# A hybrid decoder layer on one core: places in SBUF of the matmuls' two operands

## The chip, the cores and the metric

The kernel runs on one core of a Trainium2 chip. The metric is the device time of one execution in microseconds, taken as the median of several runs. PE is TensorE's matmul side, PEld its weight loads, DVE is VectorE, ACT ScalarE, POOL GpSimd and SP SyncE, which starts the transfers.

## The reference, cut to what matters

One layer is computed for 264 tokens (256 of a prompt and 8 single ones with states), all in float32:

```
xn = rms_norm(x, g_mix)                       # 2048 wide
z  = xn @ w_in                                # 3584 columns: pool 512 | lru 1024 | gelu gate 1024 | glu 512 + 512
y_pool = pool_mixer(...) @ w_pool_br          # 512 -> 2048, with a 4 x 128 x 128 map in it
y_lru  = (rg_lru(conv(u_lru)) * gelu(u_gel)) @ w_lru_br   # 1024 -> 2048, with 2 x 8 gate blocks of 128 x 128
y_conf = silu(layer_norm(conv(glu))) @ w_conf_br          # 512 -> 2048
gates  = sigmoid(xn @ w_gate + b_gate)        # 2048 -> 3 x 2048
x = x + (g_a * y_pool + g_b * y_lru + g_c * y_conf) @ w_out
x = x + square(relu(rms_norm(x, g_mlp) @ w_up)) @ w_down  # 2048 -> 8192 -> 2048
return rms_norm(x, g_final), the new states
```

## The kernel before

Tokens lie along the free axis, channels on the 128 partitions. Every product is made of k tiles: 128 input channels by 512 output columns of weights, which are four weight tiles (m = 0 to 3) of 128 x 128, against one operand tile of 128 x 264. Weights and operand are both split into a high and a low part in fp32r, and `mm3` makes each product of three matmuls (whi and x high, wlo and x high, whi and x low). So a k tile is 12 matmuls, and TensorE executes 11,405 of these and a few others.

The weights come in chunks of two k tiles (1024 floats a partition) through the ring `raw` of six. `split` writes a chunk's high part with ACT (`nc.scalar.copy`, L228) into `whi` and the rest with DVE (L229) into `wlo`, three chunks ahead of the matmuls; both hold four chunks. `weight_plan` lists 67 groups (a weight matrix, its k tiles, 512 columns) and their 478 chunks, and the main loop walks that list: it splits chunk i + 3, issues the matmuls of chunk i, evacuates the four accumulators at a group's end, and then lets `run_bg` issue work of three queues (lru, pool, conf) by a budget of cost for each engine. Everything stands in the order in which this program issues it; nothing else reorders it.

Where the operands lie is deliberate. An operand tile isn't stored in one piece: `pieces` puts its 264 columns in 33 pieces of 8 floats (32 bytes), 32 floats (128 bytes) apart, with 4 floats more after every 11 pieces. So four operand tiles fit between each other, and tile k lies `k % 4 * 8` floats to the right of the first, tiles of the next four in another set (`k // 4 * SET`, 2208 floats), the low part 1088 floats behind the high one. `both` gives the two access patterns. `turn` shifts the whole by 16 floats for each unit (for most operands 0 or 32 floats). Such tiles are `A` (the normed input, later the merged branches, and half of the MLP's hidden tiles), `L` and `LH` (the LRU's conv output, then its result), `Q` (pool and conformer results) and `xn2` (the MLP's input, four buffers; the profile calls them xn). The hidden tiles of every other quarter of the MLP lie in LH and Q.

The weight slots are 520 floats (2080 bytes) long, two for a chunk: each next k tile of weights begins 32 bytes further modulo 256. `weight_plan` picks, among the chunks of a group that are left, the first whose place fits the operand's place, `(c + turn - len(chunks)) % NHI == 0`, and the first that is left when none does. That makes the order of k in many groups a rotated one. The LRU's gate blocks (four chunks of 512 floats, kind "lru", evacuated by ACT with a sigmoid in `lru_gate_mm`, L517 and L518) and the pool's map (kind "grp") stand between the chunks of a group, at the positions that `LRU_AT` names.

Of the kernel before, what the change touches and what calls it, by code (L numbers as in the profile page):

```python
# [15 lines left out]
P = 128  # L16
# [3 lines left out]
N = TP + TS  # L20
# [27 lines left out]
STRETCH = 11  # L48
STEP = 32
HOP = STRETCH * STEP + 4  # L50
LOW = 1088
SET = 2208
SKEW = 20
A_SIZE = 8896
B_SIZE = 2496
L_SIZE = 4480
SLOT = 520
HEAD = N + 512
FIRST = 8
CH = 1024  # L60
NRAW = 6
NHI = 4
LRU_AT = (1, 3, 4, 4)
WARM = 17
LEAD = 4
SINGLE = 16
# [5 lines left out]
    return KD + c * (2 * N + CH)  # L72


def turn_of(name, k0):

    return 0 if name in ("w_in", "w_gate", "w_conf_br") else 2


def weight_plan():

    groups = [("w_in", 0, 16, m) for m in (1, 2, 0, 3, 4, 6, 5)]
    for g in range(4):
        groups += [("w_gate", 0, 16, t) for t in ((0, 4, 1), (5,), (2, 6), (3, 7))[g]]
        groups += [("w_pool_br", 0, 4, g), ("w_lru_br", 0, 8, g)]
    groups += [("w_gate", 0, 16, 8 + g) for g in range(4)]  # L90
    groups += [("w_conf_br", 0, 4, g) for g in range(4)]
    groups += [("w_out", 0, 16, m) for m in range(4)]
    for q in range(4):
        groups += [("w_up", 0, 16, q * 4 + m) for m in range(4)]
        groups += [("w_down", q * 16, 16, m) for m in range(4)]
    chunks = []
    for gi, (name, k0, k, m) in enumerate(groups):
        left, turn = list(range(k // 2)), turn_of(name, k0)
        for at in range(k // 2):
            c = next((c for c in left if (c + turn - len(chunks)) % NHI == 0), left[0])  # L100
            left.remove(c)
            chunks.append(("dense", gi, c, CH, at == 0, not left))
            for g in [g for g in range(4) if (name, m, at) == ("w_in", 4, LRU_AT[g])]:
                chunks.append(("lru", g, 0, 512))
            if (name, m) == ("w_gate", 0) and at == 3:
                chunks += [("grp", 0, 0, 512), ("none", 0, 0, 0)]
    return groups, chunks

# [2 lines left out]
def hybrid_step(ctx: ExitStack, tc: tile.TileContext, first, par_in, st_in, wall, y_out, st_out):  # L111
# [7 lines left out]


    raw = cpool.tile([P, NRAW, CH], F32, name="raw")
    whi = cpool.tile([P, 2 * NHI, SLOT], F32R, name="whi")
    wlo = cpool.tile([P, 2 * NHI, SLOT], F32R, name="wlo")
    par = cpool.tile([P, NPAR], F32, name="par")
    rstd = cpool.tile([P, N], F32, name="rstd")
    a_all = cpool.tile([P, A_SIZE], F32R, name="A")
# [15 lines left out]
        a, b = PCOL[name]  # L142
        return par[:, a:b] if i is None else par[:, a + i:a + i + n]

    def pieces(t, k, a, turn):
        at = SKEW + a + k // 4 * SET + k % 4 * OCT + turn * 2 * OCT
        return bass.AP(tensor=t.tensor, offset=t[:, at:].offset,
                       ap=[list(t.ap[0]), [HOP, N // (STRETCH * OCT)], [STEP, STRETCH], [1, OCT]])

    def high(t, k, turn=0):  # L150
        return pieces(t, k, 0, turn)

    def low(t, k, turn=0):
        return pieces(t, k, LOW, turn)

    def both(t, k, turn=0):
        return high(t, k, turn), low(t, k, turn)

    def v(t):
        return t.rearrange("p (a b c) -> p a b c", b=STRETCH, c=OCT)  # L160
# [7 lines left out]
        return psum.tile([P, 512], F32, name="acc", tag="acc")  # L168

    def w_tile(i, kt, m):  # L170
        at = 2 * (i % NHI) + kt
        return whi[:, at, m * P:(m + 1) * P], wlo[:, at, m * P:(m + 1) * P]

    spare = nc.const_aps.tensor(1.0, [P, 2 * P], dtype=mybir.dt.bfloat16)
    Gf = G.rearrange("p a n -> p (a n)")
# [45 lines left out]
    def split(j, half=None):  # L221
        if j >= len(chunks) or not chunks[j][3]:
            return
        a, b = (0, chunks[j][3] // 512) if half is None else (half, half + 1)
        at = 2 * (j % NHI)
        r = raw[:, j % NRAW, :].rearrange("p (k c) -> p k c", k=2)[:, a:b, :]
        h, lo = whi[:, at + a:at + b, :512], wlo[:, at + a:at + b, :512]
        nc.scalar.copy(h, r)  # L228
        nc.vector.tensor_tensor(lo, r, f(h), op=ALU.subtract)  # L229

    def head_half(k, h):

        s = slice(h * 256, h * 256 + 256)
        return whi[:, k, s], wlo[:, k, s], head_w(k)[:, s]

    def cast_head(k, h):
        hi, _, w = head_half(k, h)
# [116 lines left out]

    def x_high(k):
        if k < 2:
            nc.vector.tensor_scalar(high(a_all, k), v(x_of(k)), gm[:, k:k + 1], None, op0=ALU.mult)  # L357
        else:
            nc.scalar.activation(high(a_all, k), v(x_of(k)), AF.Copy, scale=gm[:, k:k + 1])

    def x_low(k):
        rest_of(both(a_all, k), x_of(k), gm[:, k:k + 1])

    def x_tile(k):
        x_high(k)
# [144 lines left out]
    def lru_gate_mm(ct, c, j):  # L510
        assert "xc" in done
        out = []
        for t in range(2):
            ps = acc()
            mm3(ps, w_tile(c, 0, 2 * j + t), both(L, ct), True, True)
            out.append(ps[:, :N])
        nc.scalar.activation(RA[:, ct, :], out[0], AF.Sigmoid, bias=pv("b_lru_a", ct))  # L517
        nc.scalar.activation(TM[:, ct, :], out[1], AF.Sigmoid, bias=pv("b_lru_x", ct))  # L518
        spend(act=1.0)
        if ct % 2:  # L520
            def times():
                nc.vector.tensor_tensor(XC[:, ct - 1:ct + 1, :], XC[:, ct - 1:ct + 1, :], TM[:, ct - 1:ct + 1, :],
                                        op=ALU.mult)
                spend(dve=0.71)

            later(1, times)
# [101 lines left out]
    def conf():  # L628
# [77 lines left out]
        stage(q, "dve", 0.3, [lambda ct=ct: affine(ct) for ct in g4])  # L706
        stage(q, "pool", 0.7, [lambda ct=ct: mul(ct) for ct in g4])
        mark(q, "swished")
        stage_split(q, 4, lambda c: both(Q(), 4 + c), lambda c: VC[:, c, :])
        mark(q, "conf")  # L710


# [16 lines left out]
    def pooling():  # L729
# [25 lines left out]
        stage("pool", "pool", 2.0, [lambda i=i: add(i) for i in range(4)])  # L755
        stage("pool", "pool", 0.3, [rows], 0)
        stage("pool", "dve", 0.8, [lambda gi=gi: diff(gi) for gi in range(4)])
        stage_split("pool", 4, lambda c: both(Q(), c, 2), lambda c: DU[:, c, :])
        mark("pool", "pool")

    def grp_mm(c):
        assert "pool" in done
        for gi in range(4):
            ps = acc()
            mm3(ps, w_tile(c, 0, gi), both(Q(), gi, 2), True, True)
            nc.scalar.activation(DU[:, gi, :], ps[:, :N], AF.Copy, scale=pv("pool_scale", gi))
        stage_split("pool", 4, lambda c: both(Q(), c, 2), lambda c: DU[:, c, :])
        mark("pool", "grp")


# [2 lines left out]
    def bpart(k):  # L773
        if not M:
            M.extend(cpool.tile([P, B_SIZE], F32R, name=f"xn2{i}", tag=f"B{i}") for i in range(4))
        return both(M[k // 4], k % 4, 2 + 2 * (k // 4 % 2))

    def gate_tile(br, g, m):
        if br == 2:
# [20 lines left out]
    def branch_evac(br, g, m, ps):  # L800
        assert "grp" in done and (br < 1 or "lru" in done) and (br < 2 or "conf" in done)
        t = gate_tile(br, g, m)
        k = g * 4 + m
        nc.vector.tensor_tensor(t, ps[:, :N], t, op=ALU.mult)
        spend(dve=0.43)
        if br == 1:
            nc.gpsimd.tensor_tensor(partial(k), t, gate_tile(0, g, m), op=ALU.add)
            spend(pool=0.8)
        if br == 2:
            nc.gpsimd.tensor_tensor(t, t, partial(k), op=ALU.add)  # L810
            spend(pool=0.8)
            later_split(*both(a_all, k, 2), t, 3, 2)

    def later_split(hi, lo, x, n, gap):
        def one():
# [39 lines left out]

    def hid(q, k):
        if q % 2 == 0:
            return both(a_all, k, 2)
        return both(LH() if k < 8 else Q(), k % 8, 2)

    def up_evac(q, m, ps):
        hi, lo = hid(q, m)
# [37 lines left out]
    def group(gi):  # L900
        name, k0, _, m = groups[gi]
        if name == "w_in":
            def rhs(i):
                return both(a_all, i)
            fn = {0: pool_evac, 1: lru_x_copy, 2: lambda c, p: lru_x_evac(4 + c, p), 3: gel_evac,
                  4: lambda c, p: gel_evac(4 + c, p), 5: ca_evac, 6: cb_evac}[m]
            return rhs, fn
        if name == "w_gate":
            return (lambda i: both(a_all, i)), (lambda c, p: gate_evac(m // 4, m % 4, c, p))
        if name == "w_pool_br":  # L910
            assert "grp" in done
            return (lambda i: both(Q(), i, 2)), (lambda c, p: branch_evac(0, m, c, p))
        if name == "w_lru_br":
            assert "lru" in done
            return (lambda i: both(LH(), i, 2)), (lambda c, p: branch_evac(1, m, c, p))
        if name == "w_conf_br":
            assert "conf" in done
            return (lambda i: both(Q(), 4 + i)), (lambda c, p: branch_evac(2, m, c, p))
        if name == "w_out":
            return (lambda i: both(a_all, i, 2)), (lambda c, p: out_evac(m * 4 + c, p))  # L920
        if name == "w_up":
            return bpart, (lambda c, p: up_evac(m // 4, (m % 4) * 4 + c, p))
        q = k0 // 16
# [2 lines left out]
    def after(gi):  # L926

        name, _, _, m = groups[gi]
        if name == "w_in":
            if m == 2:  # L930
                lru_conv(range(4, 8))
                lru_conv_sample()
                mark("lru", "conv")
                stage_split("lru", 8, lambda c: both(L, c), lambda c: XC[:, c, :])
                mark("lru", "xc")
            elif m == 5:
                conf()
# [2 lines left out]
            elif m in (3, 4):  # L940
                if m == 4:
                    gelu(0)
                    gelu(2)
                    stage_split("lru", 8, lambda c: both(LH(), c, 2), lambda c: GEL[:, c, :])
                    mark("lru", "lru")

    def by_operand(i, kt, rhs, pss):
# [22 lines left out]
    for i, ch in enumerate(chunks):  # L970
# [19 lines left out]
        if kind == "dense":  # L990
            rhs, fn = group(gi)
            name = groups[gi][0]
            start, end = ch[4:]
            if start:
                pss = [acc() for _ in range(4)]
            if i < len(chunks) - 2:
# [105 lines left out]
def _stream(w):  # L1102
    groups, chunks = weight_plan()
    out = np.zeros((len(chunks) // 2, P, 2, CH), w["w_in"].dtype)
    blocks = np.stack([w["w_lru_a"], w["w_lru_x"]], 1)
    for i, (kind, gi, c, n, *_) in enumerate(chunks):
# [75 lines left out]
```

## Time and profile before

| | us |
|---|---|
| median of 3 runs | 1321.48 (1321.29 to 1322.16) |
| the profiled execution, its own time | 1321.26 |
| its span, first to last instruction | 1319.2 |
| PE busy | 1308.6 (99%) |
| DVE busy | 841.7 (64%) |
| ACT busy | 720.1 (55%) |

A row of the timeline has the start in us from the span's start, the length of the merged instructions, engine, line, operation, output tile, then the operands and the count; matmuls of one line merge only while their operands' names stay the same, so a row changes from whi to wlo and back. Matmuls overlap in the pipeline: their length is some 0.28 us, and the distance from start to start is what the stream costs. A window's row has the length, busy time, and behind x the instructions that touch the window.

### The profile page before, as it was taken

How to read it: one execution, taken by the hardware profiler on the slowest of the kernel's cores; microseconds unless marked ns; L12 is line 12 of the kernel's file. 1: busy time of each engine (PE TensorE's matmuls, PEld its weight loads, DVE VectorE, ACT ScalarE, POOL GpSimd, SP SyncE). 2: the span in 40 equal slices, each digit the busy share in tenths (PEclk: the TensorE clock that was granted, in tenths of full speed). 3: DMA queues.
4: the chain of work that ended last, by engine and by line, in shares of the span. 5: the costliest groups of instructions: out<-in, count | busy, mean ns of one | idle time of the engine just before them, and what ended most of it. 6: DMA issues, size and time to landing. Idle time of an engine off the chain costs nothing.

```text
span 1319.2 us, 26550 instructions
## 1 busy us (share of the span) xinstructions
PE 1308.6 (99%) x11421; PEld 1306.0 (99%) x11421; DVE 841.7 (64%) x1130; ACT 720.1 (55%) x1035; POOL 100.6 (8%) x125
## 2 busy tenths in 40 slices
PE   9999999999999999999999999999999999999997
PEld 9999999999999999999999999999999999999996
DVE  8787888776777668666655455655455645465554
ACT  7668577667675645455544334543344533354544
POOL 0230010110102014021000000000000000000012
PEclk9999999999999999999999999999999999999999
DMA  8656556555575555555555555555555555555552
GB/s 330 212 192 211 173 188 224 193 192 192 192 224 192 192 192 193 192 192 192 192 192 192 192 194 192 193 194 192 193 192 193 194 195 194 192 194 195 195 193 76
DMA packets 40821, 257.48 MB, mean 195 GB/s; under 512 B 4480, under 2 KB 6784, under 8 KB 11776
## 3 DMA queue, kind: packets, MB, share of 16 engines
q1 hardware_dynamic: 40272, 255.19, 56.3%
q8 instruction: 89, 1.46, 0.4%
q10 hardware_dynamic: 432, 0.61, 0.1%
q14 instruction: 28, 0.23, 0.0%
HBM read 252.57 MB, written 3.21 MB: 194 GB/s over the span
## 4 chain that ended last, share of the span: by engine, by line
PE 97%; DVE 1%; ACT 0%; DMA 0%; issue 0%; DVEq 0%
PE acc L245 97%; DVE A L165 1%; DMA tmp<-first_dram 0%; DVE y L1068 0%; ACT whi L228 0%; DVE wlo L229 0%; DVE wlo L242 0%; ACT tmp L517 0%; DVE A L357 0%; ACT tmp L518 0%; DVE acc L1059 0%; DVEq L1159 0%; DVE G L1058 0%; DVE acc L1057 0%; PE acc L1045 0%
## 5 line engine op out<-in xcount | busy, mean ns | idle before, releaser
L229 DVE TENSOR_TENSOR wlo<-raw,whi 128x1024 fp32r<-128x1024 f32 (+1 forms) x478 | 584.7, 1226 | 454.6 <-ACT whi L228 451.3
L228 ACT CAST whi<-raw 128x1024 fp32r<-128x1024 f32 (+1 forms) x478 | 494.1, 1036 | 541.0 <-PE acc L245 495.8
L245 PE MATMUL acc<-A,whi 128*128 128x264 f32 x3968 | 679.9, 276 | 0.0
L245 PEld LDWEIGHTS acc<-A,whi 128*128 128x128 f32 x3968 | 597.1, 188 | 0.4 <-ACT whi L238 0.4
L245 PE MATMUL acc<-A,wlo 128*128 128x264 f32 x1984 | 540.9, 275 | 0.2
L245 PEld LDWEIGHTS acc<-A,wlo 128*128 128x128 f32 x1984 | 370.1, 187 | 0.9 <-DVE wlo L229 0.9
L245 PE MATMUL acc<-xn,whi 128*128 128x264 f32 x2048 | 350.9, 275 | 0.0
L245 PEld LDWEIGHTS acc<-xn,whi 128*128 128x128 f32 x2048 | 308.3, 187 | 0.0
L245 PE MATMUL acc<-xn,wlo 128*128 128x264 f32 x1024 | 280.8, 274 | 0.0
L245 PEld LDWEIGHTS acc<-xn,wlo 128*128 128x128 f32 x1024 | 191.9, 187 | 0.0
L245 PE MATMUL acc<-Q,whi 128*128 128x264 f32 x776 | 136.6, 277 | 0.0
L245 PE MATMUL acc<-LH,whi 128*128 128x264 f32 x768 | 133.3, 275 | 0.0
L245 PEld LDWEIGHTS acc<-Q,whi 128*128 128x128 f32 x776 | 118.2, 187 | 0.0
L245 PEld LDWEIGHTS acc<-LH,whi 128*128 128x128 f32 x768 | 116.4, 187 | 0.0
L245 PE MATMUL acc<-Q,wlo 128*128 128x264 f32 x388 | 107.0, 276 | 0.0
L245 PE MATMUL acc<-LH,wlo 128*128 128x264 f32 x384 | 105.3, 274 | 0.0
L854 POOL TENSOR_TENSOR G<-G 128x264 f32<-128x264 f32 x28 | 25.7, 919 | 756.6 <-ACT G L852 755.6
L245 PEld LDWEIGHTS acc<-Q,wlo 128*128 128x128 f32 x388 | 72.7, 187 | 0.0
L245 PEld LDWEIGHTS acc<-LH,wlo 128*128 128x128 f32 x384 | 71.9, 187 | 0.0
L638 ACT ACTIVATE G<-tmp,par 128x256 f32<-128x256 f32 x120 | 54.1, 500 | 3.1 <-DVE G L641 3.1
L641 DVE TENSOR_TENSOR G<-G 128x1024 f32<-128x1024 f32 x30 | 38.2, 1273 | 0.0
L887 DVE TENSOR_TENSOR X<-X,acc 128x264 f32<-128x264 f32 x79 | 28.6, 422 | 6.6 <-PE acc L245 6.6
(173 smaller groups left out, 522.6 us busy)
## 6 DMA issues: line engine op xcount, KB each, us to landing
raw<-wall_dram SPq DMA_DIRECT2D x226, 1024.0 KB, 4.8
raw<-wall_dram SPq DMA_DIRECT2D x12, 512.0 KB, 5.4
raw<-first_dram SPq DMA_DIRECT2D x6, 512.0 KB, 8.1
X<-first_dram SPq DMA_DIRECT2D x6, 264.0 KB, 7.6
raw<-wall_dram SPq DMA_DIRECT2D x5, 256.0 KB, 3.0
tmp<-first_dram SPq DMA_DIRECT2D x3, 388.0 KB, 4.8
y_dram<-y SPq DMA_DIRECT2D x3, 264.0 KB, 2.2
tmp<-st_dram SPq DMA_DIRECT2D x4, 188.0 KB, 4.9
```

The source lines that it names most:

```text
L165: nc.vector.scalar_tensor_tensor(lo, t, g, f(hi), op0=ALU.mult, op1=ALU.subtract)
L228: nc.scalar.copy(h, r)
L229: nc.vector.tensor_tensor(lo, r, f(h), op=ALU.subtract)
L245: nc.tensor.matmul(ps[:, :N], w[k == 1], x[k == 2], start=start, stop=stop)
L638: nc.scalar.activation(dst[:, ct, :TP], vext[:, ct, k:k + TP], AF.Copy, scale=par[:, w:w + 1])
L641: nc.vector.tensor_tensor(VC[:, :, :TP], VC[:, :, :TP], src[:, :, :TP], op=ALU.add)
L854: nc.gpsimd.tensor_tensor(sq2, sq2, t, op=ALU.add)
L887: nc.vector.tensor_tensor(X[:, m, :], X[:, m, :], ps[:, :N], op=ALU.add)
```

## The change

Each operand tile keeps its form (pieces of 8 floats, 128 bytes apart), but the tiles that lie between each other are now k, k + 4, k + 8 and so on in another sense: `both(t, slot, row, rows)` puts a tile in a row (1088 floats, 4352 bytes, 17 x 256) and shifts it by `slot` times 8 floats. For `A` the slot is `k // 4` and the row `k % 4`, so four successive k tiles lie under each other at one place modulo 256 bytes. For `L`, `LH` and `Q` it is `k // 2` and `k % 2`; for the MLP's input the buffer is `k % 4` and the slot `k // 4`; the hidden tiles in LH and Q change places in the same way.

A chunk of weights is written in one run of 1024 floats into a place of 1088 floats, shifted by the slot that its operand has (`slot_of`). So both k tiles of a chunk have one place modulo 256, which is the operand's slot. The chunks of a group stand in natural order of k, and there is no `turn`. `LRU_AT` now names chunks, (1, 3, 5, 6) in place of the positions (1, 3, 4, 4).

```diff
-LOW = 1088
-SET = 2208
+ROW = 1088
-SLOT = 520
+SLOT = 1088
-LRU_AT = (1, 3, 4, 4)
+LRU_AT = (1, 3, 5, 6)
...
-    return 0 if name in ("w_in", "w_gate", "w_conf_br") else 2
+    kind, gi, c = chunk[:3]
+    if kind == "lru":
+        return gi
+    if kind != "dense":
+        return 0
+    name = groups[gi][0]
+    if name in ("w_pool_br", "w_lru_br"):
+        return c
+    return 2 + c if name == "w_conf_br" else c // 2
...
-        left, turn = list(range(k // 2)), turn_of(name, k0)
-        for at in range(k // 2):
-            c = next((c for c in left if (c + turn - len(chunks)) % NHI == 0), left[0])
-            left.remove(c)
-            chunks.append(("dense", gi, c, CH, at == 0, not left))
-            for g in [g for g in range(4) if (name, m, at) == ("w_in", 4, LRU_AT[g])]:
-                chunks.append(("lru", g, 0, 512))
-            if (name, m) == ("w_gate", 0) and at == 3:
+        for c in range(k // 2):
+            chunks.append(("dense", gi, c, CH))
+            if (name, m) == ("w_in", 4) and c in LRU_AT:
+                chunks.append(("lru", LRU_AT.index(c), 0, 512))
+            if (name, m) == ("w_gate", 0) and c == 3:
                 chunks += [("grp", 0, 0, 512), ("none", 0, 0, 0)]
...
-    def pieces(t, k, a, turn):
-        at = SKEW + a + k // 4 * SET + k % 4 * OCT + turn * 2 * OCT
-        return bass.AP(tensor=t.tensor, offset=t[:, at:].offset,
-                       ap=[list(t.ap[0]), [HOP, N // (STRETCH * OCT)], [STEP, STRETCH], [1, OCT]])
-    def both(t, k, turn=0):
-        return high(t, k, turn), low(t, k, turn)
+    def both(t, slot, row, rows):
+        out = []
+        for r in (row, row + rows):
+            at = SKEW + r * ROW + slot * OCT
+            out.append(bass.AP(tensor=t.tensor, offset=t[:, at:].offset,
+                               ap=[list(t.ap[0]), [HOP, N // (STRETCH * OCT)], [STEP, STRETCH], [1, OCT]]))
+        return tuple(out)
+    def in_a(k):
+        return both(a_all, k // 4, k % 4, 4)
+    def in_half(t, k):
+        return both(t, k // 2, k % 2, 2)
...
     def w_tile(i, kt, m):
-        at = 2 * (i % NHI) + kt
-        return whi[:, at, m * P:(m + 1) * P], wlo[:, at, m * P:(m + 1) * P]
+        at = slot_of(chunks[i], groups) * OCT + kt * 512 + m * P
+        return whi[:, i % NHI, at:at + P], wlo[:, i % NHI, at:at + P]
...
-        r = raw[:, j % NRAW, :].rearrange("p (k c) -> p k c", k=2)[:, a:b, :]
-        h, lo = whi[:, at + a:at + b, :512], wlo[:, at + a:at + b, :512]
+        at = slot_of(chunks[j], groups) * OCT
+        r, h, lo = raw[:, j % NRAW, a:b], whi[:, j % NHI, at + a:at + b], wlo[:, j % NHI, at + a:at + b]
...
-        return both(M[k // 4], k % 4, 2 + 2 * (k // 4 % 2))
+        return both(M[k % 4], k // 4, 0, 1)
...
-            return both(a_all, k, 2)
-        return both(LH() if k < 8 else Q(), k % 8, 2)
+            return in_a(k)
+        return both(Q() if k % 4 // 2 else LH(), k // 4, k % 2, 2)
```

The number and the shapes of the matmuls stay as they are. Two places show what moves. The first is ACT's queue at the last two LRU gate chunks: sigmoids that empty the accumulators (tmp_71 and tmp_69 from acc), casts of weights, and the tanh of the LRU's tail (tmp_69 from tmp_71). Before:

```order
L517 ACTIVATE tmp_71<-acc,par 128x264
L518 ACTIVATE tmp_69<-acc,par 128x264
L228 CAST whi<-raw 128x2x512
L517 ACTIVATE tmp_71<-acc,par 128x264
L518 ACTIVATE tmp_69<-acc,par 128x264
L538 ACTIVATE tmp_69<-tmp_71,sp 128x264 x3
```

And after:

```order
L520 ACTIVATE tmp_71<-acc,par 128x264
L521 ACTIVATE tmp_69<-acc,par 128x264
L231 CAST whi<-raw 128x1024 x2
L520 ACTIVATE tmp_71<-acc,par 128x264
L521 ACTIVATE tmp_69<-acc,par 128x264
L541 ACTIVATE tmp_69<-tmp_71,sp 128x264 x3
```

Two casts stand between the sigmoids of the two chunks where one stood, since a dense chunk lies between them now, and a cast writes one run.

The second is TensorE where the first group of w_up goes from its first k tile to its second; xn20 and xn21 are buffers of the MLP's input. Before, both k tiles come from xn20:

```order
L245 MATMUL acc_7028<-xn20_6278,wlo_65 128x264
L245 MATMUL acc_7028<-xn20_6278,whi_64 128x264
L245 MATMUL acc_7025<-xn20_6278,whi_64 128x264
L245 MATMUL acc_7025<-xn20_6278,wlo_65 128x264
L245 MATMUL acc_7026<-xn20_6278,whi_64 128x264
```

After, the second comes from the next buffer:

```order
L248 MATMUL acc_7028<-xn20_6278,wlo_65 128x264
L248 MATMUL acc_7028<-xn20_6278,whi_64 128x264
L248 MATMUL acc_7025<-xn21_6279,whi_64 128x264
L248 MATMUL acc_7025<-xn21_6279,wlo_65 128x264
L248 MATMUL acc_7026<-xn21_6279,whi_64 128x264
```

The matmuls, their number and the weights' tiles are the same; the operand of the next k tile moved to another buffer, at the same offset in it.

More of the change, by code (lines that the diff above doesn't have):

```diff
@@ L50 @@
 HOP = STRETCH * STEP + 4
-LOW = 1088
-SET = 2208
+ROW = 1088
 SKEW = 20
-A_SIZE = 8896
+A_SIZE = 8768
 B_SIZE = 2496
-L_SIZE = 4480
-SLOT = 520
+L_SIZE = 4416
+SLOT = 1088
 HEAD = N + 512
@@ L72, in first_at, with slot_of @@
     return KD + c * (2 * N + CH)
-def turn_of(name, k0):
-    return 0 if name in ("w_in", "w_gate", "w_conf_br") else 2
+def slot_of(chunk, groups):
+    kind, gi, c = chunk[:3]
[7 more added lines that the diff above has]
+    return 2 + c if name == "w_conf_br" else c // 2
 def weight_plan():
@@ L121, in hybrid_step @@
     raw = cpool.tile([P, NRAW, CH], F32, name="raw")
-    whi = cpool.tile([P, 2 * NHI, SLOT], F32R, name="whi")
-    wlo = cpool.tile([P, 2 * NHI, SLOT], F32R, name="wlo")
+    whi = cpool.tile([P, NHI, SLOT], F32R, name="whi")
+    wlo = cpool.tile([P, NHI, SLOT], F32R, name="wlo")
     par = cpool.tile([P, NPAR], F32, name="par")
@@ L143, in pv @@
         return par[:, a:b] if i is None else par[:, a + i:a + i + n]
-    def pieces(t, k, a, turn):
-        at = SKEW + a + k // 4 * SET + k % 4 * OCT + turn * 2 * OCT
-        return bass.AP(tensor=t.tensor, offset=t[:, at:].offset,
-                       ap=[list(t.ap[0]), [HOP, N // (STRETCH * OCT)], [STEP, STRETCH], [1, OCT]])
[L150 to L154, printed above, removed]
-    def both(t, k, turn=0):
-        return high(t, k, turn), low(t, k, turn)
+    def both(t, slot, row, rows):
[9 more added lines that the diff above has]
+        return both(t, k // 2, k % 2, 2)
     def v(t):
@@ L223, in split @@
             return
-        a, b = (0, chunks[j][3] // 512) if half is None else (half, half + 1)
-        at = 2 * (j % NHI)
-        r = raw[:, j % NRAW, :].rearrange("p (k c) -> p k c", k=2)[:, a:b, :]
-        h, lo = whi[:, at + a:at + b, :512], wlo[:, at + a:at + b, :512]
+        a, b = (0, chunks[j][3]) if half is None else (half * 512, half * 512 + 512)
+        at = slot_of(chunks[j], groups) * OCT
+        r, h, lo = raw[:, j % NRAW, a:b], whi[:, j % NHI, at + a:at + b], wlo[:, j % NHI, at + a:at + b]
         nc.scalar.copy(h, r)
@@ L231, in head_half @@
     def head_half(k, h):
-        s = slice(h * 256, h * 256 + 256)
-        return whi[:, k, s], wlo[:, k, s], head_w(k)[:, s]
+        s = slice(k % 2 * 512 + h * 256, k % 2 * 512 + h * 256 + 256)
+        return whi[:, k // 2, s], wlo[:, k // 2, s], head_w(k)[:, h * 256:h * 256 + 256]
     def cast_head(k, h):
@@ L356, in x_high @@
         if k < 2:
-            nc.vector.tensor_scalar(high(a_all, k), v(x_of(k)), gm[:, k:k + 1], None, op0=ALU.mult)
+            nc.vector.tensor_scalar(in_a(k)[0], v(x_of(k)), gm[:, k:k + 1], None, op0=ALU.mult)
         else:
-            nc.scalar.activation(high(a_all, k), v(x_of(k)), AF.Copy, scale=gm[:, k:k + 1])
+            nc.scalar.activation(in_a(k)[0], v(x_of(k)), AF.Copy, scale=gm[:, k:k + 1])
     def x_low(k):
-        rest_of(both(a_all, k), x_of(k), gm[:, k:k + 1])
+        rest_of(in_a(k), x_of(k), gm[:, k:k + 1])
     def x_tile(k):
@@ L514, in lru_gate_mm @@
             ps = acc()
-            mm3(ps, w_tile(c, 0, 2 * j + t), both(L, ct), True, True)
+            mm3(ps, w_tile(c, 0, 2 * j + t), in_half(L, ct), True, True)
             out.append(ps[:, :N])
@@ L708, in conf @@
         mark(q, "swished")
-        stage_split(q, 4, lambda c: both(Q(), 4 + c), lambda c: VC[:, c, :])
+        stage_split(q, 4, lambda c: in_half(Q(), 4 + c), lambda c: VC[:, c, :])
         mark(q, "conf")
@@ L757, in pooling @@
         stage("pool", "dve", 0.8, [lambda gi=gi: diff(gi) for gi in range(4)])
-        stage_split("pool", 4, lambda c: both(Q(), c, 2), lambda c: DU[:, c, :])
+        stage_split("pool", 4, lambda c: in_half(Q(), c), lambda c: DU[:, c, :])
         mark("pool", "pool")
@@ L764, in grp_mm @@
             ps = acc()
-            mm3(ps, w_tile(c, 0, gi), both(Q(), gi, 2), True, True)
+            mm3(ps, w_tile(c, 0, gi), in_half(Q(), gi), True, True)
             nc.scalar.activation(DU[:, gi, :], ps[:, :N], AF.Copy, scale=pv("pool_scale", gi))
-        stage_split("pool", 4, lambda c: both(Q(), c, 2), lambda c: DU[:, c, :])
+        stage_split("pool", 4, lambda c: in_half(Q(), c), lambda c: DU[:, c, :])
         mark("pool", "grp")
@@ L811, in branch_evac @@
             spend(pool=0.8)
-            later_split(*both(a_all, k, 2), t, 3, 2)
+            later_split(*in_a(k), t, 3, 2)
     def later_split(hi, lo, x, n, gap):
@@ L903, in rhs @@
             def rhs(i):
-                return both(a_all, i)
+                return in_a(i)
             fn = {0: pool_evac, 1: lru_x_copy, 2: lambda c, p: lru_x_evac(4 + c, p), 3: gel_evac,
@@ L908, in group @@
         if name == "w_gate":
-            return (lambda i: both(a_all, i)), (lambda c, p: gate_evac(m // 4, m % 4, c, p))
+            return in_a, (lambda c, p: gate_evac(m // 4, m % 4, c, p))
         if name == "w_pool_br":
             assert "grp" in done
-            return (lambda i: both(Q(), i, 2)), (lambda c, p: branch_evac(0, m, c, p))
+            return (lambda i: in_half(Q(), i)), (lambda c, p: branch_evac(0, m, c, p))
         if name == "w_lru_br":
             assert "lru" in done
-            return (lambda i: both(LH(), i, 2)), (lambda c, p: branch_evac(1, m, c, p))
+            return (lambda i: in_half(LH(), i)), (lambda c, p: branch_evac(1, m, c, p))
         if name == "w_conf_br":
             assert "conf" in done
-            return (lambda i: both(Q(), 4 + i)), (lambda c, p: branch_evac(2, m, c, p))
+            return (lambda i: in_half(Q(), 4 + i)), (lambda c, p: branch_evac(2, m, c, p))
         if name == "w_out":
-            return (lambda i: both(a_all, i, 2)), (lambda c, p: out_evac(m * 4 + c, p))
+            return in_a, (lambda c, p: out_evac(m * 4 + c, p))
         if name == "w_up":
@@ L933, in after @@
                 mark("lru", "conv")
-                stage_split("lru", 8, lambda c: both(L, c), lambda c: XC[:, c, :])
+                stage_split("lru", 8, lambda c: in_half(L, c), lambda c: XC[:, c, :])
                 mark("lru", "xc")
@@ L943, in after @@
                     gelu(2)
-                    stage_split("lru", 8, lambda c: both(LH(), c, 2), lambda c: GEL[:, c, :])
+                    stage_split("lru", 8, lambda c: in_half(LH(), c), lambda c: GEL[:, c, :])
                     mark("lru", "lru")
@@ L992, in hybrid_step @@
             name = groups[gi][0]
-            start, end = ch[4:]
+            start, end = c == 0, c == groups[gi][2] // 2 - 1
             if start:
@@ L1105, in _stream @@
     blocks = np.stack([w["w_lru_a"], w["w_lru_x"]], 1)
-    for i, (kind, gi, c, n, *_) in enumerate(chunks):
+    for i, (kind, gi, c, n) in enumerate(chunks):
         if kind == "dense":
```

## The prediction

> **What bounds the kernel now.** I read the page first, then the waits of TensorE, the windows, the timeline of TensorE and the chain. The page says that TensorE is the path:
>
> ```profile
> span 1319.2 us, 26550 instructions
> PE 1308.6 (99%) x11421; PEld 1306.0 (99%) x11421; DVE 841.7 (64%) x1130; ACT 720.1 (55%) x1035; POOL 100.6 (8%) x125
> PE 97%; DVE 1%; ACT 0%; DMA 0%; issue 0%; DVEq 0%
> ```
>
> The chain of work is 97% matmuls. The waits of TensorE, all of them:
>
> ```profile
> PE acc L341 <- PEq L1153: 0.8, 1, 0.8
> PE acc L1045 <- DVE G L884: 0.3, 1, 0.3
> ```
>
> So apart from the start and the end nothing feeds TensorE too late; small delays inside a busy TensorE don't show here and are sought in the chain below. The time is the number of matmuls times the distance between their starts. (The durations of 275 ns in the groups overlap and say nothing of that distance.) The next view is the windows for TensorE; the number behind x counts also the two or three matmuls already under way at the left edge, and the column behind it is the granted clock, full everywhere. The first five stretches hold 48 matmuls each; of the four like the second, the first and the last are shown:
>
> ```profile
> 233.50:238.97 5.47, 5.47 (x50) 1.00 0.58 204
> 271.79:277.62 5.83, 5.83 (x51) 1.00 0.58 205
> ...
> 514.02:519.85 5.83, 5.83 (x50) 1.00 0.58 190
> 640.00:1040.00 400.00, 400.00 (x3512) 1.00 0.56 193
> ```
>
> The long stretch has 3510 starts in 400 us, 113.96 ns each. The edges of the first two come from the timeline, where the operand's name changes:
>
> ```profile
> 233.50 0.28 PE L245 MATMUL acc<-Q,whi 128*128 128x264 f32 x1
> 238.97 0.28 PE L245 MATMUL acc<-LH,whi 128*128 128x264 f32 x1
> 249.91 0.28 PE L245 MATMUL acc<-A,whi 128*128 128x264 f32 x1
> 271.79 0.28 PE L245 MATMUL acc<-Q,whi 128*128 128x264 f32 x1
> 277.62 0.28 PE L245 MATMUL acc<-LH,whi 128*128 128x264 f32 x1
> 288.58 0.28 PE L245 MATMUL acc<-A,whi 128*128 128x264 f32 x1
> ```
>
> Both are w_pool_br, with the same operand in Q and the same 48 matmuls: 5.47 us for g=0 and 5.83 us for g=1. The code says what differs: g=0 starts at chunk 86, its weights 128 bytes past a multiple of 256 (slot 4 of 2080 bytes), its operand 208 past one: 80 apart. g=1 starts at chunk 100: weights 0, operand 208: 208 apart, 128 more. All dense chunks that the plan could match are 80 apart (counted from the tiles' starts), eight are not, and they are the four stretches at 271.79, 392.51, 502.70 and 514.02, each 5.83 long.
>
> The second reading is what a change of k tile costs in matched chunks (timeline, rows with wlo; 12 matmuls make a k tile, and ten k tiles lie between the first row and the last):
>
> ```profile
> 684.23 0.27 PE L245 MATMUL acc<-xn,wlo 128*128 128x264 f32 x1
> ...
> 685.25 0.28 PE L245 MATMUL acc<-xn,wlo 128*128 128x264 f32 x1
> 685.59 0.27 PE L245 MATMUL acc<-xn,wlo 128*128 128x264 f32 x1
> ...
> 697.90 0.27 PE L245 MATMUL acc<-A,wlo 128*128 128x264 f32 x1
> ```
>
> Ten k tiles take 13.67 us. Inside one, the nine distances from its first wlo row to its last are 1.02 us, 113.3 ns each; the three across the change are 1.367 - 1.02 = 0.347 us, 7 ns more than 3 x 113.3. Inside a k tile weights jump by 512 bytes and between whi and wlo, and the operand between its high and low half (4352 bytes, 17 x 256): all multiples of 256, and no 7 ns. At the change both move by 32 bytes modulo 256.
>
> **The change part by part.** Sums are made against the profiled execution: 1321.26 us, of it 1319.2 span and 2.06 around it; the median of the runs is 0.22 above it.
>
> (a) Four k tiles get one place modulo 256, as do their weights, so three of four changes inside a 16-tile group move by multiples of 256 alone. In the new plan 472 dense chunks have one inner change each, and 55 groups of 16 have four chunk pairs with the same place: 472 + 220 = 692. The first six chunks wait for their data anyway (the chain, shown below, passes through VectorE and ACT until 17.42 and then stays with TensorE but for short pieces), which takes nine off: 683 x 7.0 ns = 4.8 us. Bounds: nothing, if the 7 ns belong to the new k tile and not to its place; 683 x 9 ns = 6.1, by rounding of the rows.
>
> ```profile
> 17.42 3.05 PE acc L245 x24
> ```
>
> (b) The eight unmatched chunks become matched: 4 x (5.83 - 5.47) = 1.44 us.
>
> (c) The LRU gate chunks. Their place fitted only by chance, and the last two stood together:
>
> ```profile
> 111.06 0.28 PE L245 MATMUL acc<-L,whi 128*128 128x264 f32 x1
> ...
> 112.38 0.75 PE L245 MATMUL acc<-L,whi 128*128 128x264 f32 x2
> ...
> 114.33 0.28 PE L245 MATMUL acc<-A,whi 128*128 128x264 f32 x1
> ```
>
> 24 matmuls took 3.27 us against 24 x 0.1133 = 2.72. The row at 112.38 holds the wait; the chain runs through ACT there:
>
> ```profile
> 111.26 1.05 ACT whi L228
> 112.31 0.39 ACT tmp L517
> ```
>
> ACT's sigmoids must empty the accumulators of one gate chunk before the next takes them. With a dense chunk between them (2.73 us) and matched places both parts go: 0.55, and 0.05 for the other gate chunks: 0.6 us. Bounds 0.2 (the places alone) to 0.8. The LRU chain starts two chunks later. What covers that is the distance to the first use of LH: VectorE's last LH rows end at 223.53, the use is at 238.97, 15 us against 5.5 us.
>
> ```profile
> 222.42 1.11 DVE L507 TENSOR_TENSOR LH<-tmp,LH 128x264 fp32r<-128x264 f32 x3
> ```
>
> (d) The last two chunks are interleaved and change k tile every three matmuls; all four k tiles now share a place. 45 distances: 5.32 us against 45 x 0.1133 = 5.10: 0.22 us.
>
> ```profile
> 1302.34 0.27 PE L245 MATMUL acc<-Q,wlo 128*128 128x264 f32 x1
> 1307.66 0.27 PE L245 MATMUL acc<-Q,wlo 128*128 128x264 f32 x1
> ```
>
> (e) New are jumps of both operands by -96 bytes at the end of a 16-tile group (58) and -32 (8); before, every step was +32. The trace shows no such jump. From below: no cost at all, 0.007 saved each, 0.5 in sum. From above: four k tiles run like an unmatched place, 0.36 each, 24. The nearest row is a jump out of the unmatched place: LH after it takes 288.58 - 277.62 = 10.96 us, against 249.91 - 238.97 = 10.94. I take half of these 0.02, since here both operands jump alike: 66 x 0.01 = 0.65 us lost.
>
> (f) Around 80 to 101 us VectorE is late. The weights of the chunk at 101.39 are done at 101.38, so what TensorE gains on the way there is waited away: 0.1 us lost (0 to 0.3).
>
> ```profile
> 100.17 1.21 DVE L229 TENSOR_TENSOR wlo<-raw,whi 128x1024 fp32r<-128x1024 f32 x1
> ```
>
> (g) Casts and subtractions write one run of 1024 instead of two of 512, with the same elements. They are covered: VectorE's group below sat idle for 454.6 us before its instructions, waiting for ACT's casts, which wait for TensorE to free the buffers. If that cover went, only the stretch of (f) would feel it. The changed buffers of w_up and w_down's operands move no work between engines: zero. So is the order of the weight transfers on SP, which only regroups around the LRU chunks.
>
> ```profile
> L229 DVE TENSOR_TENSOR wlo<-raw,whi 128x1024 fp32r<-128x1024 f32 (+1 forms) x478 | 584.7, 1226 | 454.6 <-ACT whi L228 451.3
> ```
>
> Sum: 4.8 + 1.44 + 0.6 + 0.22 - 0.65 - 0.1 = 6.3 us. The profiled execution would take 1315.0, the median 1321.48 - 6.3 = 1315.2 us.
>
> **The rivals.** First, the 7 ns are not of the place: a new k tile costs them wherever it lies. For it speaks that no row of a matched chunk shows a change of k tile without the 32 bytes; against it that the jumps inside a k tile, as far and farther, cost nothing. Then (a) falls out and with it (e): 1.44 + 0.6 + 0.22 - 0.1 = 2.2, time 1319.3. In the extreme addresses play no part and only the wait of (c), some 0.4 us, goes: 1321.1. The rows at 233.50 and 271.79 speak against the extreme: same names and shapes, 5.47 and 5.83.
> The Trainium skill, SBUF — State Buffer, section "SBUF: two separate sides", has the rule behind that extreme: TensorE has its own read ports, one for each operand, and never waits on anyone. By it the sum would be the 0.4 us alone; the two rows disagree with it.
>
> Second, slower: TensorE can stay in a slow rhythm although places match. After the matmul with ones at 420.24 it does:
>
> ```profile
> 420.24 0.28 PE L324 MATMUL acc<-pk,ones_r 128*128 128x264 f32 x1
> ...
> 420.48 0.29 PE L245 MATMUL acc<-A,wlo 128*128 128x264 f32 x1
> ...
> 421.57 0.28 PE L245 MATMUL acc<-A,wlo 128*128 128x264 f32 x1
> ```
>
> Nine distances take 1.09 us, 121.1 ns each, until the next k tile ends it. With the change that next step may come four k tiles later. If each of the 58 turns of (e) left TensorE so, it would cost 58 x 48 x 7.8 ns = 21.7 us against 6.95 of gains: 1336.2. It decides from 0.12 us a turn on, 15 slow matmuls of 48. Against it: after the jump at 277.62 the rhythm was back within 0.02 us.
>
> Third, the shifted LRU work makes some operand late between 114 and 240 us, by a few us; the 15 us above speak against it. 1318 to 1321.5.
>
> **How the numbers follow.** Forecast 0.80, first rival 0.10, second 0.07, third 0.03. The forecast's own range is 1313.5 to 1317: (a) with 6 to 8 ns, (e) from 0.5 gained to 1.3 lost, (c) by its bounds. The range goes up to 1319.3 for the first rival. Within 0.2% (2.6 us, about what a measurement of this kernel can tell from no change): the first rival and half of the third. Faster 0.81, same 0.11, slower 0.08.
>
> **What would show it.** (a) Ten k tiles of the timeline in 13.61 to 13.62 us instead of 13.67, and the 400 us from 640 with some 3524 starts instead of 3510. (b) The 48 matmuls of each w_pool_br and w_conf_br group in 5.45 to 5.47. (c) No row as long as that at 112.38. (e) The k tile after a turn at most 0.01 us longer than its neighbours; four k tiles at 1.45 each would be the second rival. The forecast fails if a k tile still takes 1.367, or if TensorE's waits gain a row.

## The result and the profile after

The changed kernel takes 1324.0 us (median of 12 runs, 1323.8 to 1324.85) against 1321.44 (12 runs, 1321.18 to 1322.16). The ratio is 1.0020, 95% interval 1.0011 to 1.0029: it is slower by about 2.6 us, where 6.3 us less was forecast.

The profiled execution took 1324.36 us. Its page, the lines that answer to those of before:

```profile
span 1322.6 us, 26547 instructions
PE 1310.9 (99%) x11421; PEld 1308.2 (99%) x11421; DVE 841.0 (64%) x1130; ACT 720.4 (54%) x1035; POOL 99.8 (8%) x125
PE 98%; DVE 1%; DMA 0%; issue 0%; ACT 0%; SPq 0%; DVEq 0%
```

The work of every engine is what it was and TensorE is still the chain, but it is busy 2.3 us longer. The waits of TensorE have two new rows, the second and third, both within the first 31 us:

```profile
PE acc L344 <- PEq L1156: 0.8, 1, 0.8
PE acc L248 <- DVE A L360: 0.6, 1, 0.6
PE acc L248 <- DVE wlo L232: 0.5, 1, 0.5
PE acc L1048 <- DVE G L887: 0.3, 1, 0.3
```

In the chain of waits, VectorE's and ACT's pieces end at 20.97, while the first chunks arrive (before, at 17.42):

```profile
20.97 22.32 PE acc L248 x191
```

The second group's first matmul comes at 29.17 us after and at 28.70 before, 0.22 of the 0.47 us standing already at the first group's. So the start explains little of the 3.4 us by which the span grew. The windows of TensorE find the rest. The stage w_down of the first quarter (four groups of 192 matmuls, from the first operand named A to the first named xn) takes, first before and then after:

```profile
695.05:782.57 87.52, 87.52 (x771) 1.00 0.56 193
```

```profile
695.88:783.78 87.90, 87.90 (x770) 1.00 0.57 192
695.88:718.04 22.16, 22.16 (x195) 1.00 0.57 191
718.04:739.83 21.79, 21.79 (x194) 1.00 0.57 192
701.32:707.09 5.77, 5.77 (x50) 1.00 0.61 204
723.48:728.93 5.45, 5.45 (x50) 1.00 0.53 189
```

The second and third row are its first two groups, with edges at each group's first matmul. Before, a group takes 87.52 / 4 = 21.88. Now one takes 22.16, the next 21.79, and so on in turn: two of each give 87.90. The last two rows are the second place of four k tiles (48 matmuls) in each: 5.77 us in the one and 5.45 in the other. 5.45 is 113.5 ns a matmul, 5.77 is 120.2. The second pace is called the slow rhythm here. A step is a move of both operands by 32 bytes within a group, a jump any other move that is no multiple of 256 bytes, and a turn the change from one group to the next. The timeline shows where the slow part begins:

```profile
700.87 0.39 PE L248 MATMUL acc<-A,whi 128*128 128x264 f32 x2
701.10 0.27 PE L248 MATMUL acc<-A,wlo 128*128 128x264 f32 x1
701.21 0.40 PE L248 MATMUL acc<-A,whi 128*128 128x264 f32 x2
701.45 0.29 PE L248 MATMUL acc<-A,wlo 128*128 128x264 f32 x1
701.57 0.40 PE L248 MATMUL acc<-A,whi 128*128 128x264 f32 x2
701.81 0.28 PE L248 MATMUL acc<-A,wlo 128*128 128x264 f32 x1
```

From row to row of the same kind (three matmuls) it is 0.34 us up to 701.21 and 0.36 from there. So nothing happens in the k tiles straight behind the group's turn at 695.88. The slow rhythm sets in at the first step of 32 bytes after it, and holds for the four k tiles at that place. By k tiles, in ns, worked out from the starts in the trace, this group reads 1365 1360 1360 1359, **1449 1440 1440 1440**, 1387 1360 1360 1359, 1394 1360 1360 1367, and the next one 1364 1360 1360 1361, 1366 1360 1360 1361, and so on, never over 1368. Of the 55 groups of 16 k tiles 27 are of the slow kind, and two of the four w_pool_br groups have two slow k tiles each. So 29 of the 58 turns with a jump by -96 bytes are slow. Slow and harmless turns alternate with four exceptions: the turns at 333.28 and 349.81 us and those at 393.77 and 410.30 are both slow, with a jump by -32 bytes (w_pool_br to w_lru_br) between them; those at 432.53 and 454.46 and those at 608.22 and 630.13 are both harmless, with one of the single matmuls with ones (L327, at 443.42 and 624.56) between them.

### The profile page after: what moved, and what is told of

Read it like the earlier page. It is cut to its first block, busy times and chain, and to the rows that moved or that the text cites. A ratio compares the mean times of both kernels' runs of the same rounds, so it can differ in the third digit from the quotient of the medians.

```text
span 1322.6 us, 26547 instructions
## 1 busy us (share of the span) xinstructions
PE 1310.9 (99%) x11421; PEld 1308.2 (99%) x11421; DVE 841.0 (64%) x1130; ACT 720.4 (54%) x1035; POOL 99.8 (8%) x125
## 4 chain that ended last, share of the span: by engine, by line
PE 98%; DVE 1%; DMA 0%; issue 0%; ACT 0%; SPq 0%; DVEq 0%
PE acc L248 98%; DVE A L169 0%; DMA tmp<-first_dram 0%; DVE wlo L232 0%; DVE y L1071 0%; DVE wlo L245 0%; SPq L219 0%; DVE acc L1062 0%; DVEq L1162 0%; DVE G L1061 0%; DVE acc L1060 0%; PE acc L1048 0%; PE acc L327 0%; ACT A L362 0%; ACT whi L241 0%
## 5 line engine op out<-in xcount | busy, mean ns | idle before, releaser
L248 PE MATMUL acc<-Q,whi 128*128 128x264 f32 x776 | 139.8, 275 | 0.0
L248 PE MATMUL acc<-LH,whi 128*128 128x264 f32 x768 | 138.0, 275 | 0.0
```

Of the source, the lines that this page charges most:

```text
L248: nc.tensor.matmul(ps[:, :N], w[k == 1], x[k == 2], start=start, stop=stop)
```

## The experiments

All run against the kernel before, measured beside them (1321.3 to 1321.4 us).

**e1, no jump at the turns.** Theory A: it is the jump of both operands by -96 bytes at the end of a group (places 0 1 2 3, then 0 again) that leads to the slow rhythm. Rival B: a step after four k tiles at one place can go either way. The groups' chunks are taken alternately forth and back:

```diff
+        order = list(range(k // 2))
+        ends = [slot_of(("dense", gi, c), groups) for c in (order[0], order[-1])]
+        if (name, m) != ("w_out", 0) and abs(ends[1] - place) < abs(ends[0] - place):
+            order, ends = order[::-1], ends[::-1]
+        place = ends[1]
-        for c in range(k // 2):
+        for c in order:
```

> The changed kernel, with the groups' chunks taken alternately forth and back, so that a group begins at the place where the one before ended (one jump by -96 bytes is left, ahead of w_out). Theory A (the jump by -96 bytes at a group's turn puts TensorE into a second rhythm, out of which the next step by 32 bytes leads to 120 ns a matmul): no k tiles of 1.44 us are left behind the turns, 944 k tiles at 1.36 to 1.367, and about 1314.5 us. Rival B (the jump is innocent; it is the step by 32 bytes after four k tiles at one place that can go either way): every second group or so still has four k tiles of 1.44 us, and the time stays at 1323 to 1325 us.

Measured: 1314.84 us (1314.71 to 1315.14), ratio 0.9949, interval 0.9936 to 0.9961. TensorE's windows:

```profile
516.24:538.39 22.15, 22.15 (x194) 1.00 0.55 190
691.11:712.91 21.80, 21.80 (x194) 1.00 0.55 193
640.00:1040.00 400.00, 400.00 (x3525) 1.00 0.57 194
```

The first row is the group behind the one jump that was left, w_out m=0: 22.15 us, with its 1449 1440 1440 1440. No other group has k tiles of 1.44 us; the second row is one of them. The long stretch has 3523 starts (3510 before). Theory A holds and B falls: there are as many steps after four k tiles at one place as in the changed kernel, and none goes wrong but the one behind that jump. This version beats both kernels. What is left in it is some 20 ns a group at one of the steps (a k tile of 1387).

**e2, one place for everything.** The operand is read at the first place only:

```diff
+    def read_a(k):
+        return in_a(k % 4)
-        at = slot_of(chunks[i], groups) * OCT + kt * 512 + m * P
+        at = kt * 512 + m * P
```

> The changed kernel, but every matmul of the chunks reads its operand at the first of the four places (so mostly another k tile than it should, and the result is not the reference's) with all weights written for that place: no address ever moves by anything but multiples of 256 bytes. Theory (7 ns belong to the step of place, not to the new k tile): all k tiles 1.360 us, no 120 ns interval at a change, no row of 1.44; 1312.5 to 1313.5 us. Rival (a new k tile costs 7 ns by itself): k tiles of 1.367 us and 1319 us.

```profile
640.00:1040.00 400.00, 400.00 (x3532) 1.00 0.57 195
418.42:438.58 20.16, 20.16 (x171) 1.00 0.60 212
```

In the first row there are 3530 starts, 113.31 ns each, and all k tiles take 1.360: a new k tile costs nothing by itself, and the first rival of the prediction falls. The second row contradicts what was expected: its 14 k tiles take 1.440 each, 120.0 ns a matmul, though no place changes. They lie between two single matmuls with ones, at 416.86 and 440.02 us, which read other places; ahead of the first and behind the second the pace is 113.3. Two executions took 1312.4 and 1313.0 us (the profile is of the second). Two others took 1373.2 and 1373.4, which was not expected either; e9 shows a likely cause.

**e3, one more matmul in a group.** Is the alternation one of odd and even matmuls?

```diff
+                        if gi >= 40 and (c, kt, m) == (5, 1, 0):
+                            nc.tensor.matmul(pss[m][:, :N], w_tile(i, kt, m)[1], rhs(2 * c + kt)[1], start=False,
+                                             stop=False)
```

> The changed kernel, with one matmul more (the product of the two low parts) in k tile 11 of each group from w_down 0 m=1 on, 27 groups. Theory A1 (the second rhythm is one of odd and even: it is a matter of which matmul of a pair comes first, so that one extra matmul in a group turns over what the next group does): from the group after the first extra matmul on, the groups do not alternate any more; as the first extra stands in a good group, all behind it are good, no k tile of 1.44 us after 740 us; 13 x 0.376 us gained, 27 x 0.122 lost: 1322.4 us. Rival (the alternation follows the accumulators or the count of groups): w_down and w_up go on with every second group at 1.44, and the time is 1324.0 + 3.3 = 1327.3 us.

Measured: 1327.25 us, ratio 1.0042 (1.0028 to 1.0056), the rival's time. The groups go on taking turns (first matmul to first matmul, 192 or 193 of them):

```profile
696.17:718.33 22.16, 22.16 (x194) 1.00 0.53 189
718.33:740.26 21.93, 21.93 (x195) 1.00 0.56 190
740.26:762.51 22.25, 22.25 (x195) 1.00 0.56 192
762.51:784.45 21.94, 21.94 (x196) 1.00 0.56 193
```

From the second row on each group holds the extra matmul, some 0.11 us. My theory of odd and even falls as a cause of the alternation. The extra matmul did move something: the k tile of 1394 at the last step left the slow groups and came up in the others.

**e4 and e8, term (b) alone.** In the kernel before, the weights of unmatched chunks are written 128 bytes later:

```diff
-SLOT = 520
+SLOT = 584
-        return whi[:, at, m * P:(m + 1) * P], wlo[:, at, m * P:(m + 1) * P]
+        return whi[:, at, s:s + P], wlo[:, at, s:s + P]          # s = off(i) + m * P
+    def off(i):
+        return 32 * ((chunks[i][2] + turn_of(name, k0) - i) % NHI == 2)
```

> The kernel before with only the eight unmatched chunks of w_pool_br and w_conf_br mended: their weights are written 128 bytes later, so that weights and operand are 80 bytes apart as elsewhere. Term (b) of the prediction: the four stretches of 48 matmuls take 5.47 us instead of 5.83, and the time falls by 1.44 us to 1320.0. Rival (the distance of the two places plays no part): 5.83 us as before and no gain.

e4 was built wrongly: the operand of w_conf_br lies 128 bytes further than `turn_of` tells, so that there the edit moved the four chunks that fitted. Measured: 1321.83 us, ratio 1.0002 (0.9994 to 1.0011). Its windows, two stretches mended and two spoilt:

```profile
271.78:277.38 5.60, 5.60 (x51) 1.00 0.53 190
392.25:397.85 5.60, 5.60 (x50) 1.00 0.57 186
496.73:502.63 5.90, 5.90 (x50) 1.00 0.60 218
508.47:514.36 5.89, 5.89 (x51) 1.00 0.58 198
```

The mistake is of use: the two stretches that had fitted went from 5.47 to 5.90 and 5.89 by 128 bytes alone. The same shift of the weights helps a stretch at a distance of 208 and harms one at 80, so it is the weights' place relative to the operand that counts, not their own. e8 is e4 with turn 2 in that sum for w_conf_br:

> The kernel before, and the eight unmatched chunks moved by 128 bytes; e4 did this for w_pool_br, but for w_conf_br it moved the four chunks that fitted. Now all four stretches have a distance of 80. The moved weights begin with a jump of -96 bytes modulo 256 and end with another. Theory A (every second such jump leads to 120 ns behind the next step): stretches of 5.60 us instead of 5.83, as e4 showed for w_pool_br g=1, and the two w_conf_br stretches alike: 4 x 0.23 + 4 x 0.03 = 1.0 us less, 1320.4 us. Term (b) as the prediction had it: 1320.0 us. No gain if the distance plays no part.

```profile
271.90:277.50 5.60, 5.60 (x50) 1.00 0.54 192
392.40:398.00 5.60, 5.60 (x51) 1.00 0.60 205
502.30:507.90 5.60, 5.60 (x50) 1.00 0.49 162
513.40:519.00 5.60, 5.60 (x50) 1.00 0.54 206
```

1320.42 us, ratio 0.9993 (0.9984 to 1.0002): the timing cannot tell 1 us, the four rows (edges rounded to 0.1) can, 5.60 as theory A had it. One of the eleven executions took 3518.4 us; there is no trace of it, and its cause is open. Each stretch is entered by a jump of -96 bytes and left by one. Its four k tiles read 1364 1449 1386 1401, the mark of the slow groups above; behind the jump out of it nothing happens. So e8 shows the same in a kernel in which no k tiles share a place.

**e5, jumps by +96.** From w_out on, three of four groups go back, 3 2 1 0 and then 3 again:

```diff
+        if gi >= 31 and m % 4:
+            order, ends = list(range(k // 2))[::-1], [3, 0]
```

> As e1, but from w_out on (36 groups) each stage of four groups goes forth once and then back three times: steps of -32 bytes, and two jumps by +96 a stage, 18 in all, in place of none. Theory A in its wide form (any jump by 96 bytes turns TensorE into the second rhythm, every second time): nine of the 18 jumps cost 0.37 us, 1314.8 + 3.3 = 1318.1 us. In its narrow form (only the jump by -96 does): no k tiles of 1.44 us but those behind the one jump ahead of w_out, 1314 to 1315 us.

1315.9 us, ratio 0.9958 (0.9945 to 0.9972): between the two. No k tile of 1.44 us stands behind any of the 18 jumps, but most of the steps after them take 1385 to 1407 instead of 1366, which makes the 1.1 us over e1. The narrow form holds for the slow rhythm; a jump by +96 costs some 0.06 us.

**e6, jumps inside the groups.** From w_out on a group begins at the place where the last one ended and goes upwards:

```diff
+        if gi >= 31 and m % 4:
+            order = [(2 * (4 - m % 4) + c) % 8 for c in range(8)]
+            ends = [4 - m % 4, 3 - m % 4]
```

> As e1, but from w_out on each group begins at the place where the one before ended and goes on upwards: 3 0 1 2, then 2 3 0 1, then 1 2 3 0, so that no turn of a group has a step at all and 27 jumps by -96 lie inside groups. Theory A (it is the jump that does it, wherever it stands): every second jump is followed, at the next step of 32 bytes, by four k tiles of 1.44 us: 1314.8 + 13.5 x 0.37 = 1319.8 us. Rival (the first matmuls of new accumulators together with the jump do it): no k tiles of 1.44 us inside groups, 1314.5 to 1315 us.

1320.23 us (1320.11 to 1321.18), ratio 0.9992 (0.9983 to 1.0001), close to theory A. The jumps go in turn, one slow, one without effect, counted by jumps and not by groups, for three jumps fall on four groups here. There is one exception: the jumps of w_out m=3 and w_up m=1 are both without effect, again with a matmul with ones (at 620.82 us) between them. In w_out m=2 (places 2 3 0 1) the jump stands in the middle and the step behind it leads to place 1, which the next group keeps (1 2 3 0); there is no step at that turn, and the slow rhythm lasts for eight k tiles:

```profile
580.88:592.42 11.54, 11.54 (x100) 1.00 0.46 170
```

11.54 us for 96 matmuls, 120.2 ns each. New accumulators neither start nor end it. The forecast of the time was partly luck: 12 of the 27 jumps are slow, not 13.5, but five of them are followed by eight slow k tiles instead of four.

**e7, another distance.**

```diff
-SKEW = 20
+SKEW = 16
```

> As e1, with the operands 16 bytes earlier (64 bytes behind the weights instead of 80, modulo 256). If a range of distances fits, k tiles stay at 1.36 and the time at 1314 to 1315.5 us; if only 80 fits, k tiles go to 1.44, as at the unmatched distance of 208: some 1390 us.

```profile
640.00:1040.00 400.00, 400.00 (x3333) 1.00 0.54 184
```

1387.44 us, ratio 1.0499 (1.0483 to 1.0515); 3331 starts, 120.1 ns each throughout. A distance of 64 bytes is as bad as 208. That 16 bytes cost 72.6 us against e1 is the plainest sign that addresses set TensorE's pace here. Only the operands moved, so e7 alone doesn't tell whether their distance from the weights or their own place did it.

**e9, does the slow rhythm end by itself?** e2 with one jump and one step at w_up m=2:

```diff
+        return (3, 3, 0, 0, 1)[min(c, 4)] if gi == 37 else 1     # the place of chunk c; 0 before group 37
```

> As e2 (all operands read at one place, weights written for it), with one disturbance: in the group w_up 0 m=2, which begins near 645 us, the first two chunks are read at the fourth place, the next two at the first (the jump by -96), and from the fifth chunk on everything at the second place (one step by 32), to the end. Theory (the 120 ns rhythm holds until the next step of place, of which none comes): the k tile after that step takes 1.449 us and all behind it 1.440, some 465 k tiles x 0.080 = 37 us: 1349.5 us. If the jump should be one of those that pass, 1312.5. Rival (the rhythm dies out by itself, and in the changed kernel its end after four k tiles was not due to the step): a few k tiles of 1.44, 1312.5 to 1313 us.

Five executions took 1312.1 to 1313.3 us or 1334.9 and 1335.9; the profile is of the longest. The jump by -96 that I had put in was one of those that pass: the k tiles behind it are 1360 to 1367, so the 1349.5 was missed. (Moving to the fourth place also put in a jump by +96 ahead of it.) But the rhythm showed itself elsewhere:

```profile
43.38 0.28 PE L339 MATMUL acc<-pk,ones_r 128*128 128x264 f32 x1
...
439.49 0.28 PE L339 MATMUL acc<-pk,ones_r 128*128 128x264 f32 x1
...
641.05 0.28 PE L339 MATMUL acc<-pk,ones_r 128*128 128x264 f32 x1
```

```profile
46.00:437.90 391.90, 391.90 (x3268) 1.00 0.56 188
441.00:641.00 200.00, 200.00 (x1767) 1.00 0.57 195
672.00:1072.00 400.00, 400.00 (x3532) 1.00 0.57 194
```

The single matmul with ones at 43.38, which reads other places, started it, and 3266 matmuls in a row then came 120.0 ns apart, until the next matmul with ones at 439.49. Behind that one it is 113.3. The next, at 461.39, changed nothing. The fourth, at 641.05, started it again, and the jump by +96 bytes with which the group at 669.96 begins ended it within two matmuls. In e2 the four matmuls with ones did, in their order, nothing, start, end, nothing. So the slow rhythm holds for hundreds of microseconds at a full granted clock as long as no place changes. If the two long executions of e2 were in it too, it was for 61 us / 6.7 ns, an estimated 9,100 of their 11,388 matmuls of this kind (472 chunks of 24 and five of 12; 11,405 counts 17 others with them); of these executions there is no trace.

**e10, term (c) alone.** e1 with `LRU_AT = (1, 3, 5, 5)`: the last two gate chunks side by side, with matched places.

> As e1, with the last two LRU gate chunks side by side again (after chunk 5), at matched places. If half and more of term (c) was the wait for ACT's sigmoids, the 24 matmuls of the two take some 0.4 us over 2.72; if it was the places alone, they take 2.72 to 2.73 us.

```profile
114.53:117.80 3.27, 3.12 (x26) 1.00 0.51 210
115.78 0.39 ACT tmp L525
```

The first row is TensorE's window, the second a piece of the chain of waits. One run, 1316.02 us, of which 0.8 over e1 stand already at this group's start. The 24 matmuls take 3.27 us, as long at matched places as in the kernel before at unmatched ones, with TensorE waiting for a sigmoid. So the wait alone makes the 0.55, and the places added nothing that shows there (3.266 us here, 3.269 before).

## Why the prediction was wrong

What bounds the kernel was read rightly, and four of the gains came:

- (a) 12 changes of k tile in a group at 7 ns make 0.084; a group without the slow rhythm takes 21.79 instead of 21.88, 0.09 less. e1 has 3523 starts in the long stretch, where 3524 were forecast.
- (b) was put at 1.44. The four stretches take 5.45, 5.61, 5.48 and 5.48 instead of 5.83, 1.3 less. The second has two slow k tiles:

```profile
272.94:278.39 5.45, 5.45 (x50) 1.00 0.55 189
393.77:399.38 5.61, 5.61 (x51) 1.00 0.60 209
```

- (c) was put at 0.6. The group with the gate chunks takes 27.23 us (95.40 to 122.63) instead of 28.10 (94.48 to 122.58), 0.87 less, of which 0.09 is (a): 0.78. By e10 the wait alone is 0.55 of it. The other 0.2 lies in six k tiles in and beside the gate chunks, which take 1387 to 1439 ns before and 1360 to 1367 after; of this the forecast had counted 0.05. The windows, before and after:

```profile
94.48:122.58 28.10, 28.02 (x242) 1.00 0.60 207
```

```profile
95.40:122.63 27.23, 27.23 (x242) 1.00 0.68 218
```

- (d) the last group is 0.29 shorter, 0.09 of it (a): 0.20, where 0.22 was forecast.
- (f) cost nothing in the changed kernel, which came there 0.9 us later than the one before; e1 does wait there, 0.4 us for wlo.

**The step that failed is (e).** The turns were priced at 0.01 us each, 0.65 in sum. Half of them cost nothing. 27 groups cost 22.16 - 21.79 = 0.37 each, and two stretches of w_pool_br 0.16 each: 10.3 us, sixteen times the term. One of these stretches, g=3, is already in the 1.3 of (b), which leaves 10.1 for the sum: 4.8 + 1.3 + 0.78 + 0.2 - 10.1 - 0.47 at the start = -3.5, against 3.4 us of span measured. (By the prediction's own bounds the lower end of its range would be 1313.2 instead of 1313.5.)

The price came from a single row, the jump out of the unmatched place at 277.62, where the rhythm was back at once. In e8 this is the jump that passes: of the two at such a stretch the first leads to the slow rhythm and the second does not. In the kernel before the first led into the unmatched place, where 120 ns are the rule anyway. So the one row with a visible jump was probably of the harmless kind; that is argued from e8, since in the kernel before only the operand jumps there. The bound from above, 0.36 for four k tiles, was about the true price of every second turn.

The second rival had the mechanism (a slow rhythm that holds until the next step, which now comes four k tiles later) and the price of a case (0.374). That the price fits so well is partly luck: four slow k tiles cost 0.32 us, and 0.05 more come from the steps behind them, which it didn't have. It was given 0.07 because of that same row, and for all 58 turns, 1336.2; with half of them it gives 1325.4, against 1324.0 measured. It also looked for the slow k tiles straight behind the turn, where the trace has them one place later. The first rival falls with e1 and e2, its extreme with e1 and e7 as well; the third did not happen, for TensorE's waits have no row between 114 and 240 us.

The rule of the Trainium skill (SBUF — State Buffer, section "SBUF: two separate sides"), that TensorE never waits on anyone, speaks of one engine waiting on another, and no run here tests that. Taken as the ground of the extreme rival, that addresses play no part, it does not hold: in e7 64 instead of 80 bytes between the two operands cost 72.6 us.

**What stays open.** Why about every second jump passes. It follows the count of jumps (e6), not groups, accumulators or the number of matmuls (e3), so something is carried over from one jump to the next; no run shows what. A matmul with ones or a jump by -32 bytes between two jumps stands at every exception to the alternation, but both also stand between turns that do alternate (239.84 and 421.51 us in the changed kernel), and no run tests either alone. Nor do they show why -96 and not +96 does it.

## What to carry to other kernels

When a stream of matmuls is the bound, read it in starts per stretch and by the k tile, not by its busy share: 113.3 and 120.0 ns a matmul both show as 99% busy at a full clock. When a layout repeats, price the step at which it wraps round as carefully as the steps that it saves, and from more than one row; here going forth and back removes the wrap and turns a loss of 2.6 us into a gain of 6.5. Here a disturbance that ended at the next change of place got longer when such changes got rarer, so an edit that makes a stream more even can make its faults last longer.

## What was not expected of the hardware

- TensorE has two lasting rhythms for the same kind of matmuls at the same places modulo 256 bytes, 113.3 and 120.0 ns, and stays in either: the slow one held for 3266 matmuls at granted clock 1.00 (e9).
- A single matmul that reads other places can start the slow rhythm and can end it (43.38 and 439.49 us in e9, 416.86 and 440.02 in e2) or leave the pace as it is (461.39 in e9). Executions of one program differ by up to 61 us, 1312.4 and 1373.4 for e2; that this is the cause is likely, not shown.
- In this form of operand a step of +32 bytes costs 7 ns (1.367 against 1.360 us a k tile) and in some rows up to 27 (e1), a jump of +96 some 60 ns with the steps behind it (e5), and about every second jump of -96 some 370 ns where the next step comes four k tiles later (22.16 against 21.79 us a group).
